# Who issues the stores of the second mixer's projections: SyncE, or ScalarE and GpSimd

## Chip, core and metric

The kernel runs on one core of a Trainium2 chip. The metric is the time of one execution on the device in microseconds (us), and the median over several runs is given. A profile of one execution shows every instruction of five engines: TensorE (PE, its weight loads PEld), VectorE (DVE), ScalarE (ACT), GpSimd (POOL) and SyncE (SP). An instruction that starts a transfer (DMA) stands in the queue of the engine that issues it, in that queue's order; its row carries the engine's name with a q (SPq, ACTq).

## What is computed

Two layers of a streaming encoder run over 1104 tokens: a prompt of 16 + 1024 and a sample of 64. Layer 0 mixes tokens with a gated delta rule, layer 1 with RWKV-7 time mixing; each mixer is followed by a gated feed-forward network. The change lies in layer 1's mixer, whose projections are:

```python
xx = h_prev - h
xr, xw, xk, xv, xa, xg = h[None] + xx[None] * mu[:, None, None, :]
r, k, v = xr @ w_r, xk @ w_k, xv @ w_v
w_log = -softplus(-(w0 + tanh(xw @ w1) @ w2)) - 0.5
a = sigmoid(a0 + (xa @ a1) @ a2)
gate = sigmoid(xg @ g1) @ g2
kk = l2_normalize(heads(k * k_k))
k = k * (1.0 + (a - 1.0) * k_a)
decay = exp(-exp(w_log))
...
S = S * d_t + (S @ -kk_t) * b_t + v_t * k_t      # token by token, in the kernel by chunks of 64
bonus = sum(r * k * r_k, heads) * v
```

All is float32; a product of matrices is made of three passes over a high and a low part of each operand.

## The kernel before

Activations lie with the 1024 channels on 8 tiles f of 128 partitions and tokens along the row, in three groups g of 336, 384 and 384 tokens (`FULL`). The mixer has two halves. `rwkv_a` computes the projections and writes them, one tile of 128 x 384 per (f, g), to scratch tensors in DRAM: R, SW (the sigmoid that gives the decay), A, PQ (running decay), KR (two planes: scaled kk and scaled r), BK (two planes: scaled a*kk and k), V, BV (bonus) and GT (gate). `rwkv_b` reads them back by batches of heads and runs the chunked recurrence.

The stages of `rwkv_a` in order:

- `dense(0)`: receptance, with `store` writing R (L1265). VectorE copies the tile out of PSUM for odd f, ScalarE for even f. Woven into it run the low-rank projections `lora`; their second stage writes SW (L1252) and A (L1265), both made by ScalarE.
- `dense(2)` with `post_k`: per tile it loads A (L1391) and SW (L1401), normalises the key with one more matmul (L1405), scans the decay on VectorE (L1414), makes three exponentials on ScalarE (pe, pi, pq: L1416 to L1418), copies a column block of pq on GpSimd (plb, L1419), and stores PQ (L1421), KR[0] (L1423), BK[0] (L1426) and BK[1] (L1428). The last three are VectorE's products pe, bh, kh. Their tiles have two buffers each.
- `dense(3)` with `post_v`: per tile it loads PQ, BK[1] and R (L1455 to L1457), multiplies on VectorE (rt L1458, kh L1460), sums per head with a matmul (L1462), copies V out of PSUM on ScalarE (L1464), multiplies it (pq, L1466), and stores KR[1] (L1459), V (L1465) and BV (L1467). pq, kh and rt have two buffers each, and so has ev. Woven into it run the first steps of the recurrence's first batch: `grams`, `inverse` (a substitution whose columns VectorE and GpSimd share, L599 and L601; transposes L1602, L1605 after it) and `build` (loads L1553 to L1556).
- `gates`: loads the gate's hidden rows (L1150), four matmuls per tile (L1166), a copy on ScalarE (go, L1168, two buffers), and the store GT (L1169). All but its start runs beside the first batch of `rwkv_b`.

`mix` (L1219 to L1240) makes the shifted input of each projection and splits it into high and low part; GpSimd writes one column (md, L1236) where the sample starts. Weights come by `wunit` (L117), 512 KB each.

In the text of the kernel every one of these loads and stores is issued by `nc.sync`. The order of instructions on each queue is not the program's: a planner orders them by priorities and its own estimate of durations, and adds the semaphores. `weave(*gens)` only interleaves the program order of several generators by given weights.

Of the kernel before, what the change touches and what calls it, by code (L numbers as in the profile page):

```python
# [11 lines left out]
AF = mybir.ActivationFunctionType  # L12
# [40 lines left out]
def tile_trunk(ctx, tc, *aps, stages=("gdn", "ffn0", "rwkv", "ffn1"), dbg=None):  # L53
    nc = tc.nc
# [1088 lines left out]
    def gates(tp, xp, dr):  # L1143
        w2 = ins["rwkv_g2"][0]
        hid = []
        for i in range(3):
            t = tp.tile([P, T], F32R, tag=f"hg{i}", bufs=1, name=uid("hg"))
            for c0, n in FULL:
                x = xp.tile([P, 384], F32, tag="ev", name=uid("hx"))
                nc.sync.dma_start(x[:, :n], dr["HG"][i, :, c0:c0 + n])  # L1150
                nc.scalar.copy(t[:, c0:c0 + n], x[:, :n])
            yield
            hid.append(t)
        raws = [rep2(w2[0:128], 1), rep2(w2[128:160], 4)]
        h, l, h2 = (tp.tile([P, KT, P], F32R, tag=f"g2{i}", bufs=1, name=uid("g2")) for i in range(3))
        split(h.rearrange("p a b -> p (a b)"), l.rearrange("p a b -> p (a b)"), raws[0])
        hf = h2.rearrange("p a b -> p (a b)")
        nc.scalar.copy(hf, raws[1])
        nc.vector.tensor_tensor(hf[64:128], raws[1][64:128], hf[64:128].bitcast(F32), ALU.subtract)
        terms = [(h, hid[0]), (h, hid[1]), (l, hid[0]), (h2, hid[2])]  # L1160
        yield
        for f in range(8):
            for g, (c0, n) in enumerate(LIVE):
                ps = psC()
                for i, (w, x) in enumerate(terms):
                    nc.tensor.matmul(ps[:, :n], w[:, f], x[:, c0:c0 + n], start=i == 0, stop=i == 3)  # L1166
                o = tp.tile([P, 384], F32, tag="go", bufs=2, name=uid("go"))
                nc.scalar.copy(o[:, :n], ps[:, :n])  # L1168
                nc.sync.dma_start(dr["GT"][f, :, (g + 1) * 384 - n:(g + 1) * 384], o[:, :n])  # L1169
                yield  # L1170

    def hand_over(tp, xT, c0, n):
# [23 lines left out]
    def rwkv_a(hnp, col, prm, pc, plb, dr, esb, esx, esg, pend, esP):  # L1196
        C = math.exp(-0.5)
        with ExitStack() as es0, ExitStack() as es:
# [4 lines left out]
            o = pc["rwkv_mu"]  # L1203
            nc.vector.tensor_scalar(omu, prm[:, o:o + 48], -1.0, 1.0, ALU.mult, ALU.add)
            ka1 = rp.tile([P, 8], F32, name="ka1")
            o = pc["rwkv_k_a"]
# [35 lines left out]
            def store(ps, n, g, f, name, func=AF.Copy, bias=0.0):  # L1242
                if name == "SW":
                    i = 2 if g else 1
                    e = (sv1 if g else sv0)[cnt[i] % 2]
                    cnt[i] += 1
                    if g == 0:
                        nc.scalar.activation(e[:, 0, 49:65], ps[:, 0:16], func, bias=bias)
                        nc.scalar.activation(e[:, 1:6, 1:65], ps[:, 16:n].rearrange("p (c t) -> p c t", t=64), func, bias=bias)
                    else:  # L1250
                        nc.scalar.activation(e[:, :, 1:65], ps[:, :n].rearrange("p (c t) -> p c t", t=64), func, bias=bias)
                    nc.sync.dma_start(dr["SW"][f, :, 6 * g:6 * g + 6], e)  # L1252
                else:
                    if g == 0:
                        e = ev0[cnt[0] % 2]
                        cnt[0] += 1
                    else:
                        e = mp.tile([P, 384], F32, tag="ev", name=uid("ev"))
                    if func == AF.Copy and f % 2:
                        nc.vector.tensor_copy(e[:, 384 - n:], ps[:, :n])  # L1260
                    elif func == AF.Copy:
                        nc.scalar.copy(e[:, 384 - n:], ps[:, :n])
                    else:
                        nc.scalar.activation(e[:, 384 - n:], ps[:, :n], func, bias=bias)
                    nc.sync.dma_start(dr[name][f, :, g * 384:(g + 1) * 384], e)  # L1265

            def dense(s, w, post):
                m = [None] * 3
# [128 lines left out]
            def post_k(ps, n, g, f):  # L1397
                o = 384 - n
                A = load("l0", "A", f, g)
                sw = tmp("sw", [P, 390])  # L1400
                nc.sync.dma_start(sw, dr["SW"][f, :, 6 * g:6 * g + 6].rearrange("p a b -> p (a b)"))  # L1401
                sq = tmp("sq")
                nc.scalar.activation(sq[:, :n], ps[:, :n], AF.Square, scale=col("rwkv_k_k", f))
                pn = psC()
                nc.tensor.matmul(pn[:, :n], bd1, sq[:, :n], start=True, stop=True)  # L1405
                nc.scalar.activation(sq[:, :n], pn[:, :n], AF.Ln, bias=eps_t)
                nc.scalar.activation(sq[:, :n], sq[:, :n], AF.Exp, scale=-0.5)
                kk, k2 = (kk0[f % 2], k20[f % 2]) if g == 0 else (tmp("kk"), tmp("k2"))
                nc.vector.scalar_tensor_tensor(kk[:, o:], ps[:, :n], col("rwkv_k_k", f), sq[:, :n], ALU.mult, ALU.mult)
                nc.scalar.activation(k2[:, o:], A[:, o:], AF.Identity, scale=col("rwkv_k_a", f), bias=ka1[:, f:f + 1])  # L1410
                nc.vector.tensor_tensor(k2[:, o:], k2[:, o:], ps[:, :n], ALU.mult)
                nc.vector.tensor_tensor(A, A, kk, ALU.mult)
                l = sw.rearrange("p (c t) -> p c t", t=65)
                nc.vector.tensor_tensor_scan(sw, sm.rearrange("p a b -> p (a b)"), sw, 0.0, ALU.mult, ALU.add)  # L1414
                pe, pi, pq = tmp("pe"), tmp("pi"), tmp("pq")
                nc.scalar.activation(c3(pe), l[:, :, 0:64], AF.Exp, scale=-C)  # L1416
                nc.scalar.activation(c3(pi), l[:, :, 1:65], AF.Exp, scale=C)
                nc.scalar.activation(c3(pq), l[:, :, 1:65], AF.Exp, scale=-C)  # L1418
                nc.gpsimd.tensor_copy(plb[:, f, 6 * g:6 * g + 6], c3(pq)[:, :, 63])  # L1419
                cs = slice(g * 384, (g + 1) * 384)  # L1420
                nc.sync.dma_start(dr["PQ"][f, :, cs], pq)  # L1421
                nc.vector.tensor_tensor(pe, kk, pe, ALU.mult)
                nc.sync.dma_start(dr["KR"][0, f, :, cs], pe)  # L1423
                bh, kh = tmp("bh"), tmp("kh")
                nc.vector.tensor_tensor(bh, A, pi, ALU.mult)
                nc.sync.dma_start(dr["BK"][0, f, :, cs], bh)  # L1426
                nc.vector.tensor_tensor(kh, k2, pi, ALU.mult)
                nc.sync.dma_start(dr["BK"][1, f, :, cs], kh)  # L1428

            for i, (dst, c) in enumerate(((p_shift, SPL), (s_shift, T))):  # L1430
                t8 = tp.tile([P, 8], F32, tag="t8", bufs=1, name=f"t8{i}")
# [13 lines left out]
            with ExitStack() as es, ExitStack() as es1:  # L1445
                set_wp(es, 2, 3)
                mp = pool(es, "rm3", 2)
                mdb[0] = 2
                mp0 = pool(es1, "rm0", 2)

                def post_v(ps, n, g, f):
                    o = 384 - n
                    cs = slice(g * 384, (g + 1) * 384)
                    pq, kh, rt = (mp.tile([P, 384], F32, tag=t, name=uid(t)) for t in ("pq", "kh", "rt"))
                    nc.sync.dma_start(pq, dr["PQ"][f, :, cs])  # L1455
                    nc.sync.dma_start(kh, dr["BK"][1, f, :, cs])
                    nc.sync.dma_start(rt, dr["R"][f, :, cs])  # L1457
                    nc.vector.tensor_tensor(rt, rt, pq, ALU.mult)  # L1458
                    nc.sync.dma_start(dr["KR"][1, f, :, cs], rt)  # L1459
                    nc.vector.scalar_tensor_tensor(kh, rt, col("rwkv_r_k", f), kh, ALU.mult, ALU.mult)  # L1460
                    pn = psC()
                    nc.tensor.matmul(pn[:, :384], bd1, kh, start=True, stop=True)  # L1462
                    e = ev0[f % 2] if g == 0 else mp.tile([P, 384], F32, tag="ev", name=uid("ev"))
                    nc.scalar.copy(e[:, o:], ps[:, :n])  # L1464
                    nc.sync.dma_start(dr["V"][f, :, cs], e)  # L1465
                    nc.vector.tensor_tensor(pq, pn[:, :384], e, ALU.mult)  # L1466
                    nc.sync.dma_start(dr["BV"][f, :, cs], pq)  # L1467

                d = dense(3, ins["rwkv_w_v"][0], post_v)
                for _ in range(4):  # L1470
                    next(d)
                Bx.home(flat(hnp.rearrange("p a b -> p (a b)")))
                weave((8, upto(8, d)), (D1, then(Bx.grams(0), Bx.inverse(0))))
                weave((8, upto(8, d)), (D2, Bx.build(0, 0)))
                es1.close()
                gts = gates(pool(esg, "rg", 2, side="right"), mp, dr)
                weave((4, d), (4, upto(4, gts)))
            return Bx, gts
# [399 lines left out]
    if "gdn" in stages:  # L1878
        dr = {k: dp_.tile([9, P, 8, P], F32, name="d" + k) for k in ("KN", "VB", "KD", "QG", "TT", "QK", "SZ")}
        dr["G"] = dp_.tile([9, 8, P], F32, name="dG")  # L1880
        with ExitStack() as es:
# [4 lines left out]
            with ExitStack() as es2:  # L1886
# [14 lines left out]
                with lnexp_tables():  # L1901
                    load_x(xT, ready)
                    nc.sync.dma_start(dx, xT)
                    for g in range(3):
                        n = FULL[g][1]
# [103 lines left out]
```

## Time and profile before

| | |
|---|---|
| median of 3 runs | 3351.06 us (3349.12 to 3355.72) |
| profiled execution | 3353.38 us, span 3351.6 us |
| granted TensorE clock, mean | 0.974 |
| instructions | 69660 |
| moved by DMA | 452.49 MB, mean 135 GB/s |
| share of the busiest queue (q1) | 445.61 MB |

The span is the time from the first to the last instruction of the profile. The stages that the diff touches lie between about 1598 and 2160 us. Busy time of an engine counts its own instructions, not waits and not the issuing of DMAs. A wait row names the waiting instruction, what ended the wait, the total in us, how many times, and the longest. In a row of one source line, durations are in ns as minimum/median/maximum, then first and last start in us.

### The profile page before, as it was taken

How to read it: one execution, taken by the hardware profiler on the slowest of the kernel's cores; microseconds unless marked ns; L12 is line 12 of the kernel's file. 1: busy time of each engine (PE TensorE's matmuls, PEld its weight loads, DVE VectorE, ACT ScalarE, POOL GpSimd, SP SyncE). 2: the span in 40 equal slices, each digit the busy share in tenths (PEclk: the TensorE clock that was granted, in tenths of full speed). 3: DMA queues.
4: the chain of work that ended last, by engine and by line, in shares of the span. 5: the costliest groups of instructions: out<-in, count | busy, mean ns of one | idle time of the engine just before them, and what ended most of it. 6: DMA issues, size and time to landing. Idle time of an engine off the chain costs nothing. (4 is left out here: it accounts for less than half of the span.)

```text
span 3351.6 us, 69660 instructions
## 1 busy us (share of the span) xinstructions
PE 3177.9 (95%) x27426; PEld 2983.6 (89%) x27426; DVE 2505.8 (75%) x5011; ACT 1561.5 (47%) x3134; POOL 293.1 (9%) x539
## 2 busy tenths in 40 slices
PE   7999999898999999999999888888999999999998
PEld 6888888798999999999998777677778999999998
DVE  6967867467777667766879874889986687877775
ACT  5866766434433333213778733434455443333112
POOL 1000000002200000000001130533300310000000
PEclk9999999999999999999999999989999999999999
DMA  5433332884332225422256876445565333335231
GB/s 167 118 99 101 105 91 71 293 278 138 97 98 82 78 75 169 131 83 88 76 184 194 279 227 211 134 141 164 161 192 170 105 97 97 94 94 175 85 98 61
DMA packets 543912, 452.49 MB, mean 135 GB/s; under 512 B 78377, under 2 KB 494930, under 8 KB 543458
## 3 DMA queue, kind: packets, MB, share of 16 engines
q1 hardware_dynamic: 538682, 445.61, 43.2%
q8 instruction: 216, 3.54, 0.4%
q10 hardware_dynamic: 4904, 2.43, 0.3%
q14 instruction: 110, 0.90, 0.1%
HBM read 306.86 MB, written 141.07 MB: 134 GB/s over the span
## 5 line engine op out<-in xcount | busy, mean ns | idle before, releaser
L311 PE MATMUL psA<-tc,sh 128*128 128x276 f32 (+1 forms) x1712 | 500.2, 292 | 20.4 <-DVE hs L319 9.4
L313 PE MATMUL psA<-tc,sl 128*128 128x276 f32 (+1 forms) x1712 | 499.9, 292 | 4.0 <-DVE sl L110 3.9
L312 PE MATMUL psA<-tc,sh 128*128 128x276 f32 (+1 forms) x1712 | 499.4, 292 | 0.3 <-DVE tc L110 0.2
L407 DVE TENSOR_TENSOR xT<-xT,psA 128x384 f32<-128x384 f32 (+3 forms) x496 | 252.4, 521 | 135.0 <-PE psA L132 133.2
L311 PEld LDWEIGHTS psA<-tc,sh 128*128 128x128 f32 x1712 | 327.0, 191 | 22.6 <-DVE hs L319 10.1
L109 ACT CAST wh<-raw 128x1024 fp32r<-128x1024 f32 x159 | 166.3, 1049 | 357.8 <-PE psA L131 239.9
L313 PEld LDWEIGHTS psA<-tc,sl 128*128 128x128 f32 x1712 | 326.5, 191 | 5.0 <-DVE sl L110 4.7
L312 PEld LDWEIGHTS psA<-tc,sh 128*128 128x128 f32 x1712 | 326.6, 191 | 1.2 <-DVE tc L110 0.9
L131 PE MATMUL psA<-hl,wh 128*128 128x384 f32 (+3 forms) x1024 | 326.4, 319 | 0.0
L130 PE MATMUL psA<-hh,wh 128*128 128x384 f32 (+3 forms) x1024 | 325.7, 320 | 0.0
L132 PE MATMUL psA<-hh,wl 128*128 128x384 f32 (+3 forms) x1024 | 325.3, 318 | 0.0
L130 PE MATMUL psA<-hnh,wh 128*128 128x384 f32 (+1 forms) x768 | 269.9, 351 | 5.4 <-ACT hnh L109 4.1
L131 PE MATMUL psA<-hnl,wh 128*128 128x384 f32 (+1 forms) x768 | 262.3, 341 | 1.7 <-DVE hnl L110 1.7
L132 PE MATMUL psA<-hnh,wl 128*128 128x384 f32 (+1 forms) x768 | 261.0, 340 | 0.0
L110 DVE TENSOR_TENSOR wl<-raw,wh 128x1024 fp32r<-128x1024 f32 x159 | 195.0, 1228 | 66.0 <-ACT wh L109 65.5
L109 ACT CAST sh<-raw 128x512 fp32r<-128x512 f32 x202 | 124.9, 621 | 254.9 <-PE psA L312 235.0
L130 PE MATMUL psA<-mxh,wh 128*128 128x384 f32 (+1 forms) x672 | 225.0, 345 | 10.6 <-ACT mxh L109 5.6
L131 PE MATMUL psA<-mxl,wh 128*128 128x384 f32 (+1 forms) x672 | 229.7, 344 | 1.9 <-DVE mxl L110 1.6
L132 PE MATMUL psA<-mxh,wl 128*128 128x384 f32 (+1 forms) x672 | 226.8, 339 | 0.3 <-DVE wl L110 0.3
L130 PEld LDWEIGHTS psA<-hh,wh 128*128 128x128 f32 x1024 | 192.0, 188 | 0.6 <-ACT hh L109 0.4
L132 PEld LDWEIGHTS psA<-hh,wl 128*128 128x128 f32 x1024 | 192.4, 188 | 0.1
L131 PEld LDWEIGHTS psA<-hl,wh 128*128 128x128 f32 x1024 | 192.2, 188 | 0.3
(490 smaller groups left out, 8204.3 us busy)
## 6 DMA issues: line engine op xcount, KB each, us to landing
raw<-in_ffn_w_gate_dram SPq DMA_DIRECT2D x64, 512.0 KB
raw<-in_ffn_w_up_dram SPq DMA_DIRECT2D x64, 512.0 KB
raw<-in_ffn_w_down_dram SPq DMA_DIRECT2D x44, 512.0 KB
raw<-in_gdn_w_in_dram SPq DMA_DIRECT2D x32, 512.0 KB
raw<-in_gdn_w_out_dram SPq DMA_DIRECT2D x24, 512.0 KB
raw<-in_rwkv_w_o_dram SPq DMA_DIRECT2D x24, 512.0 KB
hr<-dhid SPq DMA_DIRECT2D x44, 276.0 KB
hr<-dhid SPq DMA_DIRECT2D x44, 272.0 KB
```

The costliest lines, as they stand in the source:

```text
L109: nc.scalar.copy(h, src)
L110: (eng or nc.vector).tensor_tensor(l, src, h.bitcast(F32), ALU.subtract)
L130: nc.tensor.matmul(ps, w[0][:, k, :], x[0][:, k, :n], start=a, stop=False)
L131: nc.tensor.matmul(ps, w[0][:, k, :], x[1][:, k, :n], start=False, stop=False)
L132: nc.tensor.matmul(ps, w[1][:, k, :], x[0][:, k, :n], start=False, stop=z)
L311: nc.tensor.matmul(ps, u[0][:, kk], h, start=first and kk == 0, stop=False)
L312: nc.tensor.matmul(ps, u[0][:, kk], l, start=False, stop=False)
L313: nc.tensor.matmul(ps, u[1][:, kk], h, start=False, stop=last and kk == 3)
L407: nc.vector.tensor_tensor(xT[:, m, a:a + n], xT[:, m, a:a + n], pd[:, :n], ALU.add)
```

## The change

Only the engine that issues a store is changed, in `gates`, `store`, `post_k` and `post_v`; no load, tile or computation is. Stores of tiles that ScalarE wrote go to ScalarE's queue: GT, SW, A, R of even f, PQ, V. Stores of VectorE's tiles go to GpSimd's queue: KR[0], BK[0], BK[1], KR[1], BV. R of odd f, which VectorE copies, stays with SyncE.

```diff
@@ gates
-                nc.sync.dma_start(dr["GT"][f, :, (g + 1) * 384 - n:(g + 1) * 384], o[:, :n])
+                nc.scalar.dma_start(dr["GT"][f, :, (g + 1) * 384 - n:(g + 1) * 384], o[:, :n])
@@ store
-                    nc.sync.dma_start(dr["SW"][f, :, 6 * g:6 * g + 6], e)
+                    nc.scalar.dma_start(dr["SW"][f, :, 6 * g:6 * g + 6], e)
...
-                    if func == AF.Copy and f % 2:
+                    q = nc.sync if func == AF.Copy and f % 2 else nc.scalar
+                    if q is nc.sync:
                         nc.vector.tensor_copy(e[:, 384 - n:], ps[:, :n])
...
-                    nc.sync.dma_start(dr[name][f, :, g * 384:(g + 1) * 384], e)
+                    q.dma_start(dr[name][f, :, g * 384:(g + 1) * 384], e)
@@ post_k
-                nc.sync.dma_start(dr["PQ"][f, :, cs], pq)
+                nc.scalar.dma_start(dr["PQ"][f, :, cs], pq)
                 nc.vector.tensor_tensor(pe, kk, pe, ALU.mult)
-                nc.sync.dma_start(dr["KR"][0, f, :, cs], pe)
+                nc.gpsimd.dma_start(dr["KR"][0, f, :, cs], pe)
                 bh, kh = tmp("bh"), tmp("kh")
                 nc.vector.tensor_tensor(bh, A, pi, ALU.mult)
-                nc.sync.dma_start(dr["BK"][0, f, :, cs], bh)
+                nc.gpsimd.dma_start(dr["BK"][0, f, :, cs], bh)
                 nc.vector.tensor_tensor(kh, k2, pi, ALU.mult)
-                nc.sync.dma_start(dr["BK"][1, f, :, cs], kh)
+                nc.gpsimd.dma_start(dr["BK"][1, f, :, cs], kh)
@@ post_v
-                    nc.sync.dma_start(dr["KR"][1, f, :, cs], rt)
+                    nc.gpsimd.dma_start(dr["KR"][1, f, :, cs], rt)
...
-                    nc.sync.dma_start(dr["V"][f, :, cs], e)
+                    nc.scalar.dma_start(dr["V"][f, :, cs], e)
                     nc.vector.tensor_tensor(pq, pn[:, :384], e, ALU.mult)
-                    nc.sync.dma_start(dr["BV"][f, :, cs], pq)
+                    nc.gpsimd.dma_start(dr["BV"][f, :, cs], pq)
```

## The prediction

> **What bounds the kernel now.** I read the page's head, its queue part and its chain first.
>
> ```profile
> span 3351.6 us, 69660 instructions
> q1 hardware_dynamic: 538682, 445.61, 43.2%
> PE 30%; DVE 6%; DMA 1%; issue 1%; ACT 1%; POOL 0%; SPq 0%; DVEq 0%; ACTq 0%; POOLq 0%
> ```
>
> TensorE carries the chain (PE 30%). Nearly all bytes (445.61 MB) go through one queue, q1, which is SyncE's. No row shows a transfer that GpSimd issued. Over the whole span SP's own issuing (SPq) is 0% of the chain, so the stages that the diff touches decide. The view of busy time by windows gives them: length, then busy us (and counts) of PE, PEld, DVE, ACT, POOL, then granted clock, DMA share, GB/s.
>
> ```profile
> 1598.00:1765.00 167.00, 160.55 (x915) 153.80 (x914) 134.50 (x273) 124.61 (x268) 13.58 (x38) 0.99 0.41 131
> 1765.00:1895.00 130.00, 118.54 (x628) 105.75 (x625) 120.16 (x224) 111.33 (x233) 19.11 (x33) 0.99 0.73 236
> 1895.00:2062.00 167.00, 148.01 (x1149) 127.14 (x1150) 112.44 (x223) 65.01 (x128) 33.71 (x70) 0.93 0.79 243
> 2062.00:2160.00 98.00, 84.56 (x1544) 70.03 (x1543) 71.64 (x171) 42.00 (x99) 31.71 (x71) 0.89 0.48 136
> ```
>
> In order: receptance and low-rank stage (PE-bound); key stage (DVE busy 120.16 of 130); value stage (PE idle 19.0); gates with the first batch (PE idle 13.4). All PE idle together is 50.3 us (562 less 511.65), the most that any relief could bring. Next, the waits inside these windows: who waited, for what, total us, times, longest.
>
> ```profile
> PE psC L1462 <- DVE kh L1460: 10.5, 8, 2.3
> PE psA L130 <- ACT wh L109: 4.8, 1, 4.8
> DVE rt L1458 <- DMA pq<-rPQ: 13.8, 7, 5.1
> DVE sw L1414 <- DMA sw<-rSW: 3.5, 4, 1.5
> ```
>
> The first three are of the value stage: PE waits for kh, kh for rt, rt for the load of pq. The last is the key stage's. So a late load costs something in the value stage, little before it.
>
> **The change, part by part.** It takes 252 stores off SP: 132 to ScalarE (GT 24, SW 24, A 24, PQ 24, V 24, R of even f 12) and 120 to GpSimd (KR 48, BK 48, BV 24). R of odd f, 12 stores, stays on SP. Bytes and loads stay. Prices of one issue, from the rows of single lines (min/median/max ns, first and last start) and of the timeline:
>
> ```profile
> L1169 SPq DMA_DIRECT2D rGT<-go x24: 319/537/1442, 2060.9 to 2155.4; - x24
> 581.04 0.51 ACT L225 ACTIVATE sg<-sg 128x384 f32<-128x384 f32 x1
> 581.17 0.37 ACTq L972 DMA_DIRECT2D dTT<-tfp  x1
> 581.58 0.53 ACT L226 ACTIVATE sg<-sg 128x384 f32<-128x384 f32 x1
> ```
>
> *Relief of SP, value stage start.* PE stands 4.8 us at the first weight. SP reached that load only after the wait of a PQ store:
>
> ```profile
> 1887.95 0.42 SPq L1391 DMA_DIRECT2D l<-rA  x1
> 1890.04 0.32 SPq L1421 DMA_DIRECT2D rPQ<-pq  x1
> 1890.41 0.43 SPq L117 DMA_DIRECT2D raw<-in_rwkv_w_v_dram  x1
> ```
>
> From 1888.4 (end of the load) to 1890.4 SP stood or issued that store: 2.0 us. Ends: 0, if the raw tile's memory was not free, and 4.8. I take 2.0, the row's own: **-2.0**.
>
> *Relief, value stage loop.* SP's own waits there:
>
> ```profile
> SPq L1459 <- DVE rt L1458: 13.0, 12, 3.1
> SPq L1465 <- ACT ev L1464: 10.2, 11, 2.2
> SPq L1467 <- DVE pq L1466: 9.1, 10, 3.1
> SPq L1455 <- DMA rBV<-pq: 6.5, 12, 1.1
> ```
>
> SP stands 32.3 us before the three stores, and loads queue behind. But at 12 of the 24 loads of pq SP itself was waiting for the BV store to leave the buffer (two buffers): these cannot come earlier. So half of PE's 10.5 us is out of reach; of the other 5.2 I take half, **-2.6** (ends 0 and -5.2).
>
> *Relief, key stage.* DVE, its bound, waits 3.5 us for sw; a third, **-1.2** (ends 0 and -3.5). In the low-rank stage PE is busy 160.55 of 167, and no load of it stands among the waits above: 0 (at most the 6.4 us of PE's idle time there).
>
> *Relief, gates.* SP issues nearly back to back, GT stores among the loads; the chain of waits runs through it:
>
> ```profile
> 2147.99 1.44 SPq L1169 DMA_DIRECT2D rGT<-go  x1
> ...
> 2060.92 2.90 DMA rGT<-go
> 2078.31 3.25 DMA k<-rKR
> 2149.47 0.57 SPq L1553
> 2150.09 0.61 SPq L1553
> 2150.75 3.47 DMA xT<-rKR
> ```
>
> 24 issues at the median 0.537 give SP 12.9 us back. On the chain stand 10.8 us of transfer and issue (the five rows); a transfer's own time stays, so the gain is what SP was late: the store of 1.44 ahead of 2149.47, and I put as much again for the other two places: **-3.0** (ends 0 and -10.8).
>
> *ScalarE's 132 issues.* Each costs at most 0.37 and a turnaround that I put at 0.1, where nothing else runs, and next to nothing where an instruction runs meanwhile (the issue at 581.17 lies inside L225, which ends at 581.55; the next starts at 581.58). At a mean 0.2, 60 stores (SW, A, R) put 12 us on ACT's 124.6 of 167, and 24 PQ stores 5 us on 111.3 of 130: covered by PE's 160.6 and DVE's 120.2, though tightly. **+2.5** for copies that come a little later on the chain (ends 0, and 132 x 0.47 = 62 on ACT, of which the key stage would pass DVE by 111.3 + 11.3 - 120.2 = 2.4 and the low-rank stage 0). ACT writes these tiles itself, so its stores wait only for ACT; nothing foreign blocks its queue.
>
> *GpSimd's 120 stores.* One such store's price on POOL is shown nowhere. Ends: 0.32 (the shortest of SP's row) and 2.06, POOL's longest row in these stages. The nearest is an instruction of POOL's own over 128 partitions, 1.03, and I take that.
>
> ```profile
> L1419 POOL COPY plb<-pq x24: 193/403/2056, 1768.2 to 1891.3; 128x6 f32<-128x6 f32 x24
> L1419 POOL COPY plb<-pq 128x6 f32<-128x6 f32 x24 | 14.2, 594 | 119.9 <-ACT pq L1418 119.9
> L1236 POOL TENSOR_TENSOR md<-prm 128x1 f32<-128x1 f32 x16 | 7.7, 481 | 39.2 <-DVE mxl L110 39.0
> L1598 POOL MEMSET b32t<- 128x1024 f32 x2 | 2.1, 1026 | 15.8 <-DVE b32tn L1605 13.4 <-DMA rBK<-kh 2.4
> L1427 DVE TENSOR_TENSOR kh<-k,pi x24: 547/551/556, 1784.8 to 1896.7; 128x384 f32<-128x384 f32 x24
> ```
>
> Key stage: a round takes (1896.7 - 1784.8)/23 = 4.87 us. POOL's round becomes 3 x 1.03 + 0.59 (plb) + 0.32 (md, 7.7/24) = 4.0: covered, **0**. POOL becomes the bound from (4.87 - 0.91)/3 = 1.32 us a store; each 0.1 above costs 0.1 x 3 x 23 = 6.9 us. The last round's stores leave about 1.7 us later (3 x (1.03 - 0.45)), and the value stage reuses that memory (POOL's MEMSET L1598 already waits 2.4 us for rBK<-kh): **+1.5** (ends 0 and 3 x 1.6 = 4.8). The md columns of both stages (16) queue behind stores that wait for DVE: **+1.0** (ends 0 and 16 x 1.03).
>
> Value stage: BV and KR[1] sit on rings of two buffers; each of 11.5 turns grows by 1.03 - 0.32 = 0.7. Half of them bind (12 of 24 above): **+4.1** (ends -1, as stores no longer queue on SP, and 11.5 x 1.74 = 20). The Trainium skill, DMA: Bandwidth & Descriptors, Specifications, gives a first byte after about 1 us for a GpSimd store against 0.6 for SyncE's or ScalarE's; by that 0.4 this term would be 2.3, and no run here shows it yet. POOL also does part of the first inverse in this stage:
>
> ```profile
> L599 POOL TENSOR_TENSOR b32w<-b32a,b32t x158: 228/468/767, 1946.4 to 2426.4; 128x27 f32<-128x27 f32 x10, 128x52 f32<-128x52 f32 x10, 128x75 f32<-128x75 f32 x10, 128x96 f32<-128x96 f32 x10
> 1971.77 0.24 POOL L601 TENSOR_TENSOR b32t<-b32t,b32w 128x23 f32<-128x23 f32 x1
> 1981.11 0.17 DVE L601 TENSOR_TENSOR b32t<-b32t,xT 128x8 f32<-128x8 f32 x1
> L1458 DVE TENSOR_TENSOR rt<-rt,pq x24: 544/557/837, 1904.9 to 2052.9; 128x384 f32<-128x384 f32 x24
> ```
>
> POOL starts it at 1946.4 and ends 9.3 us before DVE's part. Rounds of (2052.9 - 1904.9)/23 = 6.4 us put 4 rounds, 8 stores, 8.2 us, into it: just covered. **+1.0** for stores that hold POOL while DVE makes rt and pq (ends 0 and 8 x 2.06 - 9.3 = 7.2); when late, DVE's transpose L1602 and PE behind it stand.
>
> *Sum.* -2.0 - 2.6 - 1.2 - 3.0 = -8.8; +2.5 + 1.5 + 1.0 + 4.1 + 1.0 = +10.1; together +1.3. The profiled execution took 3353.4 (span 3351.6 and 1.8 around it): 3354.7. It lies 2.3 above the median of 3351.1, so the forecast for the median is **3352.4: no measurable change**. A difference under 0.2%, 6.7 us, cannot be told from none here.
>
> **Rivals.** *Faster: the stores were what made the loads late.* If GpSimd's stores leave as soon as SP's did and ACT hides its own, the costs vanish and the relief doubles: half of PE's 15.3 us in the value stage (7.7), all 3.5 of the key stage, half the 10.8 of the gates: -16.6, 3334. SP's waits of 32.3 us speak for it; the 12 loads that wait for a landing speak against. Chance 0.26.
>
> *Slower: the ring of two buffers in the value stage.* A BV store that lands later makes the load of pq, rt, kh and PE's L1462 later at every turn. With all turns bound and 1.5 us a store: 11.5 x 1.18 = 13.6 instead of 4.1, and the loop's relief of 2.6 gone: +13.4, 3364.5. It decides (past +6.7) from 0.92 us if every turn binds. For it: PE's 10.5 us wait is this very chain; against: half the turns have slack. Chance 0.18.
>
> *Slower: POOL becomes the key stage's bound.* At 1.6 us a store, 2.8 x 6.9 = +19.3: 3372. POOL's plb copies, 193 ns at best and 594 on average beside a DVE that is 92% busy, show that POOL is held up there. Chance 0.18. The Trainium skill, SBUF — State Buffer, SBUF: two separate sides, says that a GpSimd store's descriptors cannot be written while VectorE holds the shared port, and a later section there has 620 ns alone and about 3100 beside a tensor_copy; at 3.1 us this rival would be +123. The same page, Who interferes with whom, exempts tensor_tensor, which is most of what DVE runs here, so I give the long price little weight.
>
> *The change moves more than it says.* Queues are not filled in program order: R's stores, the first stage's, still run 20 us after the key stage's first loads.
>
> ```profile
> L1265 SPq DMA_DIRECT2D rR<-ev x24: 319/320/1073, 1598.5 to 1766.9; - x24
> L1401 SPq DMA_DIRECT2D sw<-rSW x24: 320/442/1205, 1746.6 to 1886.0; - x24
> ```
>
> So the planner may place other work anew; I count that both ways inside the range, and as no case of its own.
>
> **Chances.** The forecast keeps 0.38, and is the "same" case; faster 0.26; slower 0.18 + 0.18 = 0.36. The range goes down to 3336, nearly the faster rival, and up to 3376, past both slower ones; the forecast's own range is 3344.4 to 3357.8.
>
> **What would show it.** SP's waits at L1459, L1465 and L1467 gone, PE's first weight of the value stage earlier by about 2 us, SP less dense after 2062. POOL rows of DMA issue with a duration: under 1.32 us the key stage keeps 130 us, above it grows. PE's wait for kh in the value stage: under 10.5 us the ring did not bind, above 15 it did. POOL's last L601 of the first inverse before DVE's. I am wrong if a POOL store takes 1.5 us or more, or if ACT's issues make PE wait in the first stage.

## The result: 1.3% slower

The changed kernel took 3391.27 us (median; 3387.0 to 3395.3) against 3350.09 for the kernel before on the same chip: ratio 1.013, 95% interval 1.0114 to 1.0146. The prediction, 3352.4 with a range up to 3376, was wrong, and both of its slower rivals were too small.

From here on, lines after L1259 carry a number one higher in the changed kernel: its L1266 is L1265 before, its L1468 is L1467. The head of its page, queues and chain:

```profile
span 3393.2 us, 69701 instructions
q1 hardware_dynamic: 502394, 396.24, 38.5%
q10 hardware_dynamic: 23912, 28.21, 2.4%
q0 software_dynamic: 7680, 23.60, 1.8%
PE 28%; DVE 8%; issue 4%; DMA 3%; POOL 2%; ACT 1%; SPq 0%; DVEq 0%; ACTq 0%; POOLq 0%
```

The change did what it says: q1 lost 49.4 MB (445.61 before), and ScalarE's q10 and GpSimd's q0 carry it. In the chain POOL went from 0% to 2%, DMA from 1% to 3%, issue from 1% to 4%.

Where the time went is seen best in a table by stage. I cut both spans at the same events: ScalarE's first copy of R, the first key matmul (L1405), the first value matmul (L1462), the first gate matmul (L1166), the last one, the end. The view by windows, before and then after (columns as in the prediction):

```profile
1597.20:1780.30 183.10, 173.35 (x984) 165.40 (x983) 148.29 (x301) 139.38 (x300) 13.97 (x39) 0.98 0.42 132
1780.30:1909.10 128.80, 116.64 (x603) 103.83 (x602) 118.66 (x217) 105.56 (x218) 22.12 (x39) 0.96 0.78 253
1909.10:2056.00 146.90, 134.09 (x1100) 115.51 (x1098) 98.25 (x196) 53.44 (x107) 28.52 (x58) 0.97 0.77 236
2056.00:2152.20 96.20, 81.50 (x1433) 66.73 (x1434) 67.35 (x161) 41.99 (x97) 27.82 (x62) 0.89 0.50 145
2152.20:3351.60 1199.40, 1135.92 (x11492) 1069.65 (x11492) 934.29 (x1859) 463.97 (x894) 144.51 (x258) 0.97 0.41 124
```

```profile
1600.50:1805.30 204.80, 182.11 (x985) 172.60 (x984) 148.26 (x300) 143.81 (x298) 13.79 (x39) 0.93 0.37 118
1805.30:1946.30 141.00, 118.72 (x581) 104.12 (x580) 115.89 (x212) 102.45 (x212) 59.01 (x112) 0.91 0.69 226
1946.30:2117.00 170.70, 144.29 (x1120) 124.02 (x1118) 99.53 (x202) 57.85 (x115) 53.25 (x104) 0.92 0.70 217
2117.00:2208.70 91.70, 77.13 (x1434) 63.77 (x1430) 67.87 (x162) 42.31 (x97) 29.20 (x63) 0.93 0.58 169
2208.70:3393.00 1184.30, 1121.95 (x11493) 1058.11 (x11492) 931.38 (x1858) 462.59 (x893) 148.07 (x258) 0.98 0.40 123
```

Receptance stage +21.7, key stage +12.2, value stage +23.8, gates -4.5, all behind them -15.1; the part ahead of the first cut, where nothing differs, +3.3. Together 41.4 of the spans' 41.6.

Read the first row of each block. Three engines are less busy per microsecond after, and no engine is the bound: 182.11 of 204.80 on PE, 148 on DVE, 144 on ACT. Time that no engine uses is waiting, so the next view is PE's waits for `mxh` from 1590 to 1790 us, before and after (the stage after runs on to 1805, and has 15.8 us in all):

```profile
PE psA L130 <- ACT mxh L109: 2.9, 3, 1.5
```

```profile
PE psA L130 <- ACT mxh L109: 15.0, 8, 4.1
```

The matmuls stand before `mxh`, ScalarE's cast of the mixed input. Why it is late is in ScalarE's timeline just ahead of the worst wait (PE stands 4.1 us up to 1685.1):

```profile
1682.10 0.58 ACT L1251 ACTIVATE sv<-psA,prm 128x384 f32<-128x384 f32 x1 [0.17 <-DMA rSW<-sv]
1683.55 0.58 ACT L1251 ACTIVATE sv<-psA,prm 128x384 f32<-128x384 f32 x1 [0.87 <-DMA rSW<-sv]
1683.61 0.88 ACTq L1252 DMA_DIRECT2D rSW<-sv  x2
1684.53 0.51 ACT L109 CAST mxh<-md 128x384 fp32r<-128x384 f32 x1 [0.40 <-ACT sv L1251]
```

The cast that PE needs stands behind a run of `sv` sigmoids. The two shown wait until the store of an earlier one has left its buffer (0.17 and 0.87 us), and the cast then waits 0.40 us while ScalarE issues a store. That is 1.4 of the 4.1 us; in the rest ScalarE works through other instructions that stand ahead of the cast. Nor did the waits for those buffers grow: they are 1.5 us in the stage, before and after. Two causes are mixed here: the order in which the instructions stand, and the issues. The program asks for the same instructions in both; the planner placed 385 of TensorE's 22198, 310 of VectorE's 5011 and 230 of ScalarE's 3131 elsewhere (the fewest moves that turn one order into the other).

A hole here can cost more than its own length. PE's idle time in the stage grew from 9.75 us (183.10 less 173.35) to 22.69, by 12.9; the other 8.8 us is the same matmuls taking longer, 182.11 against 173.35, at a granted clock of 0.93 instead of 0.98. By windows of 5 us around two holes (PE idle 4.14 us up to 1685.1 and 3.50 up to 1703.1):

```profile
1680.00:1685.00 5.00, 0.83 (x3) 0.31 (x3) 1.24 (x3) 3.06 (x8) 0.00 (x0) 0.95 0.74 242
1685.00:1690.00 5.00, 4.91 (x15) 4.51 (x16) 4.93 (x11) 3.40 (x8) 0.00 (x0) 0.50 0.11 42
1690.00:1695.00 5.00, 5.00 (x29) 5.00 (x29) 3.73 (x9) 2.58 (x6) 0.81 (x2) 0.87 0.00 0
...
1700.00:1705.00 5.00, 1.88 (x5) 1.58 (x6) 2.35 (x6) 4.21 (x12) 0.26 (x1) 0.66 0.46 169
1705.00:1710.00 5.00, 5.00 (x22) 4.84 (x21) 5.00 (x13) 3.46 (x8) 1.54 (x4) 0.66 0.00 2
```

After the first hole the clock is 0.50, and 15 matmuls start in a window where the next one has 29 at 0.87. The Trainium skill, TensorE: Matmul & The Clock Gate, Part 1: The HAM clock gate, says that the clock falls to half after an idle window of about 3.4 us and comes back after as long a busy one; this trace agrees, with 0.50 behind that hole of 4.14 us.

In the key stage PE waits for `sq`, ScalarE's square of the key, before and after:

```profile
PE psC L1405 <- ACT sq L1403: 4.7, 5, 1.6
```

```profile
PE psC L1406 <- ACT sq L1404: 14.7, 12, 4.1
```

That is 10.0 of the stage's 12.2 us.

The value stage has its own mechanism. Rows of VectorE, GpSimd, SyncE and TensorE around its longest hole:

```profile
1992.44 0.55 DVE L1467 TENSOR_TENSOR pq<-psC,ev 128x384 f32<-128x384 f32 x1
...
2001.10 0.44 POOL L599 TENSOR_TENSOR b32w<-b32a,b32t 128x143 f32<-128x143 f32 x1
2001.57 0.58 POOL L1468 DMA_DIRECT2D rBV<-pq  x1
2002.17 0.47 POOL L601 TENSOR_TENSOR b32t<-b32t,b32w 128x143 f32<-128x143 f32 x1
...
2003.77 0.32 SPq L1456 DMA_DIRECT2D pq<-rPQ  x1
...
2006.18 0.56 DVE L1459 TENSOR_TENSOR rt<-rt,pq 128x384 f32<-128x384 f32 x1 [6.01 <-DMA pq<-rPQ]
2007.15 0.81 DVE L1461 SCALAR_TENSOR_TENSOR kh<-rt,prm,kh 128x384 f32<-128x384 f32 x1
2008.02 1.65 PE L1463 MATMUL psC<-kh,bd 128*128 128x384 f32 x2 [7.52 <-DVE kh L1461]
```

`pq` was ready at 1992.99. Its store left GpSimd at 2001.57, 8.6 us later, between two column steps of the inverse; GpSimd works through its queue in order and had a row of them ahead. SyncE could load the next `pq` into that buffer only at 2003.77, so rt, kh and TensorE followed, with a hole of 7.5 us. Over the stage SyncE's wait for BV to land, 6.5 us before (the prediction's row of L1455), became:

```profile
SPq L1456 <- DMA rBV<-pq: 36.0, 15, 7.5
```

Pairing the 24 products with the 24 stores in order of time, three BV stores left 8.6, 11.4 and 6.2 us after their data and the others within 2.3; of KR[1] three left 8.8, 8.4 and 3.7 us after, the others within 2.9. Before, the longest such delay was 0.8 for BV and 3.2 for KR[1].

### The profile page after: what moved, and what is told of

The parts are those of the page before. It is cut to its first block, busy times and chain, and to the rows that moved or that the text cites. A ratio compares the mean times of both kernels' runs of the same rounds, so it can differ in the third digit from the quotient of the medians.

```text
span 3393.2 us, 69701 instructions
## 1 busy us (share of the span) xinstructions
PE 3184.3 (94%) x27426; PEld 2988.4 (88%) x27426; DVE 2501.7 (74%) x5011; ACT 1564.9 (46%) x3134; POOL 359.4 (11%) x659
## 5 line engine op out<-in xcount | busy, mean ns | idle before, releaser
L109 ACT CAST sh<-raw 128x512 fp32r<-128x512 f32 x202 | 124.6, 619 | 254.8 <-PE psA L312 233.8
L132 PEld LDWEIGHTS psA<-hh,wl 128*128 128x128 f32 x1024 | 192.5, 188 | 0.1
```

The costliest lines, as they stand in the source:

```text
L109: nc.scalar.copy(h, src)
L132: nc.tensor.matmul(ps, w[1][:, k, :], x[0][:, k, :n], start=False, stop=z)
```

## Experiments

Two theories: **P**, the planner's new order of the compute instructions takes the time; **H**, the stores cost it on their new queues. To separate them I hold the order. The planner takes edges that fix the order of issue and add no wait, so the instructions of TensorE, VectorE, ScalarE and GpSimd can be made to stand as in another kernel:

```python
# names: the compute instructions of one engine, in the other kernel's order
for ins, prev in zip(names[1:], names):
    tc.add_manual_dep(here[ins], prev, NoSync)      # issue order only
```

DMAs are not held, and so SyncE's own order still changes: in `p_after_queues` 264 of its DMAs stand elsewhere than before (counted as above). No run holds a kernel to its own order, so what holding itself does is not measured. The table gives the median, the ratio to the kernel before with its interval, and the lengths of the stages in the one profile of each kernel.

| kernel | us | ratio (95%) | receptance | key | value | gates | rest |
|---|---|---|---|---|---|---|---|
| before | 3349 to 3352 | 1 | 183.1 | 128.8 | 146.9 | 96.2 | 1199.4 |
| changed | 3391.3 | 1.013 (1.0114-1.0146) | 204.8 | 141.0 | 170.7 | 91.7 | 1184.5 |
| p_after_queues | 3368.9 | 1.0062 (1.0044-1.0079) | 192.2 | 127.7 | 161.4 | 92.0 | 1198.6 |
| p_before_queues | 3402.2 | 1.0175 (1.0152-1.0198) | 200.9 | 155.9 | 159.5 | 102.6 | 1187.0 |
| e_act | 3360.5 | 1.0041 (1.0024-1.0058) | 203.0 | 133.1 | 152.4 | 91.1 | 1190.4 |
| e_pool | 3365.4 | 1.0050 (1.0031-1.0069) | 185.2 | 132.8 | 179.7 | 90.8 | 1191.3 |
| p_kr1bv_sp | 3355.1 | 1.0010 (0.9999-1.0020) | 193.0 | 128.3 | 152.9 | 90.6 | 1191.0 |
| p_first_sp | 3359.2 | 1.0031 (1.0020-1.0043) | 183.1 | 128.7 | 160.9 | 91.6 | 1198.1 |
| p_kr1bv_act | 3359.7 | 1.0033 (1.0020-1.0046) | 192.5 | 128.8 | 156.6 | 91.1 | 1193.0 |
| e_gt | 3336.0 | 0.9950 (0.9936-0.9964) | 182.9 | 128.2 | 152.2 | 94.8 | 1186.9 |
| p_gt | 3343.2 | 0.9988 (0.9975-1.0001) | 181.8 | 128.8 | 148.6 | 94.5 | 1190.7 |
| b_gtorder | 3364.6 | 1.0052 (1.0033-1.0070) | 183.8 | 128.4 | 149.3 | 123.4 | 1193.5 |
| g_pqv | 3343.2 | 0.9986 (0.9974-0.9999) | 181.4 | 130.3 | 155.0 | 91.1 | 1189.1 |
| g_key | 3340.5 | 0.9975 (0.9961-0.9988) | 182.2 | 129.2 | 154.3 | 90.7 | 1189.8 |
| a_hold1 | 3387.8 | 1.0106 (1.0088-1.0125) | 192.5 | 146.0 | 172.7 | 90.4 | 1187.9 |
| e_ra | 3357.4 | 1.0025 (1.0012-1.0037) | 186.6 | 130.3 | 149.2 | 94.5 | 1197.4 |
| e_sw | 3368.6 | 1.0061 (1.0041-1.0081) | 201.5 | 129.0 | 144.3 | 96.3 | 1195.7 |

How far to trust one stage: in the kernels with no edit in it, receptance lies between 181.4 and 185.2, value (no store of the key or value stage moved, and their order as before) between 144.3 and 152.2, and the rest between 1184 and 1199. The part ahead of the stages, where no store was moved, ends between 1590.8 and 1601.1. And a profile shows one execution, which need not be a middling one: `e_pool`'s took 3379.2 us against a median of 3365.4, `b_gtorder`'s 3373.1 against 3364.6, `e_gt`'s 3343.2 against 3336.0, `e_sw`'s 3359.3 against 3368.6.

**Order against queues.** `p_after_queues`: the full change, compute held to the order before.

> The changed kernel with its stores on ScalarE's and GpSimd's queues, but the order of all compute instructions on TensorE, VectorE, ScalarE and GpSimd held to that of the kernel before (ordering edges only). SyncE's loads and the places of the stores stay the planner's. Theory P (the planner put the compute instructions in another order, and that order costs the 41 us): 3345 to 3362 us, and the receptance stage is back within 5 us of before's. Theory H (the stores cost what they cost on their new queues: issue time, waits in front of them, later landings): 3380 to 3395, with the receptance stage still some 20 us longer and the value stage some 20 us longer. In between: both, in the measure of where it lies.

`p_before_queues`: no store moved, compute held to the order of the full change.

> The mirror image: all stores stay with SyncE as in the kernel before, but the compute instructions of the four engines are held to the order that the planner made for the changed kernel. Theory P: 3380 to 3400 us, with the receptance stage some 20 us longer than before's. Theory H: 3345 to 3358, no measurable change.

Neither end was hit by the first: 3368.9 lies between, so both causes are there. The second gave 3402.2 with every store still on SyncE: the order alone is enough for a loss of this size (SyncE's order goes with it: 332 of its 1744 DMAs stand elsewhere than before). PE's waits for `mxh` in the receptance stage, of `p_before_queues` and then `p_after_queues`:

```profile
PE psA L130 <- ACT mxh L109: 13.8, 6, 4.1
```

```profile
PE psA L130 <- ACT mxh L109: 6.4, 9, 3.2
```

With the new order and no store on ScalarE it is 13.8 us; with the old order and the stores there 6.4; before 2.9. ScalarE's timeline in `p_before_queues`, and then at the same place in the kernel before:

```profile
1685.94 0.58 ACT L1251 ACTIVATE sv<-psA,prm 128x384 f32<-128x384 f32 x1 [1.21 <-DMA rSW<-sv]
1687.27 0.58 ACT L1251 ACTIVATE sv<-psA,prm 128x384 f32<-128x384 f32 x1 [0.74 <-DMA rSW<-sv]
...
1690.03 0.58 ACT L1251 ACTIVATE sv<-psA,prm 128x384 f32<-128x384 f32 x1 [0.33 <-DMA rSW<-sv]
1690.51 0.50 ACT L109 CAST mxh<-md 128x384 fp32r<-128x384 f32 x1
```

```profile
1689.17 1.06 ACT L1251 ACTIVATE sv<-psA,prm 128x384 f32<-128x384 f32 x2
...
1691.09 0.94 ACT L109 CAST mxh<-md 128x384 fp32r<-128x384 f32 x2
1692.28 1.13 ACT L1251 ACTIVATE sv<-psA,prm 128x384 f32<-128x384 f32 x2
...
1693.75 0.50 ACT L109 CAST mxh<-md 128x384 fp32r<-128x384 f32 x1
```

In the new order the cast that PE wants stands behind a run of sigmoids and other work and comes at 1690.51, where a hole of 3.8 us ends (1691.06). Waiting for the `sv` buffers is the smaller part of it: of the three waits shown only the last, 0.33 us, falls into the hole. In the old order the casts stand between pairs of sigmoids.

The key stage's whole loss goes with the order (127.7 held, 141.0 not; PE's wait for `sq` is 4.2 us held), the value stage's only in part (161.4). A held order has a price of its own, though: it was made for other queues. The last hole of `p_before_queues`, 14.3 us in the gates, is in neither kernel, so its total is no measure of the order to the microsecond.

**Half the change each.** `e_act`: ScalarE's 132 stores. `e_pool`: GpSimd's 120. The planner is free in both.

> Only ScalarE's 132 stores moved (GT, SW, A, R of even f, PQ, V); the 120 of VectorE's tiles stay with SyncE. The planner orders freely. Theory H with ScalarE's issues as the cost in the receptance stage and GpSimd's stores as the cost in the key and value stages: receptance stage +20, key and value stage within 5 of before's, gates some 5 shorter: 3360 to 3368. Theory P: 356 of TensorE's 22198 instructions stand elsewhere than before, nearly as many as in the full change (385), so also the key and value stages are longer: 3370 to 3390.

> Only GpSimd's 120 stores moved (KR, BK, BV); the 132 of ScalarE's tiles stay with SyncE. The planner orders freely. Theory H: receptance stage as before, key stage +12 and value stage +24 as in the full change: 3380 to 3390. Theory P: 220 of TensorE's instructions stand elsewhere; the time is set by where, and lies below that of the full change: 3350 to 3375.

Receptance +20 with ScalarE's stores alone and +2 with GpSimd's, value stage +5.5 and +32.8 (of these +5.5 is hardly outside the spread, and +32.8 is from an execution 14 us over its median). The receptance loss comes with ScalarE's stores and most of the value loss with GpSimd's, as H had it by stage, though with a free planner this does not part issues from order; of the totals `e_act`'s is in H's range, `e_pool`'s in P's. The key stage lost only 4 us in each, 12 in both together.

**Which stores, at a fixed order.** `p_after_queues` with KR[1] and BV on SyncE (`p_kr1bv_sp`), with the receptance stage's stores on SyncE (`p_first_sp`), or with KR[1] and BV on ScalarE (`p_kr1bv_act`):

> The changed kernel with compute held to the order before, as in p_after_queues (3368.9 us, value stage 161.4 us against 146.9 before), but KR[1] and BV, the two stores of the value stage, back on SyncE. Theory Q (on GpSimd these two stand behind the column steps of the inverse, leave late, and the loads into the same two-buffer tiles wait for their landing: SyncE waited 33.5 us for BV and 28.2 for KR there, against 6.5 and 3.1 before): value stage back within 4 us of 146.9, SyncE's two waits under 12 us, total 3352 to 3360. Rival (it is the planner's new order of SyncE's loads, or the key stage's late stores): value stage stays over 155, total 3363 to 3372.

> The changed kernel with compute held to the order before, but the 60 stores of the receptance stage (SW, A, R of even f) back on SyncE. Receptance stage: 192.2 us in p_after_queues, 183.1 before. Theory A (ScalarE's issues and the wait of its sv for the SW landing delay the mxh casts): back to 182 to 186, TensorE's wait for mxh from 6.4 back to 2.9 us, total 3358 to 3364. Rival (order of SyncE's loads): stays near 192, total 3365 to 3372.

> As p_kr1bv_sp, but KR[1] and BV on ScalarE's queue instead of SyncE's, so still off SyncE and not behind GpSimd's inverse. Theory Q: value stage 140 to 150 us, total 3350 to 3360. Rival (any store that leaves SyncE lets the loads and stores of one ring lose their order, whichever engine takes it): value stage over 155, total 3363 to 3372.

The clearest result is `p_first_sp`: 183.1 us, exactly before's stage, and the wait for `mxh` at 2.6. So at the old order ScalarE's 60 stores cost 9 us. The order of SyncE's loads, the rival, is out: apart from the 60 stores, one DMA of SyncE stands elsewhere than in `p_after_queues`. `p_kr1bv_sp` brought 3355.1, no longer told from before, with the value stage at 152.9 (2 us over what was expected, and 0.7 over the spread of the kernels without an edit there); 32 of SyncE's other DMAs stand elsewhere than in `p_after_queues`. On ScalarE the two stores give the total that theory Q asked, 3359.7, but the stage of its rival, 156.6. No KR[1] or BV store stood over 3 us behind its data in it. What remains there I cannot assign.

One expectation was badly made. SyncE's two waits for a landing were to fall under 12 us in `p_kr1bv_sp`; the one for BV stayed at 14.7, the one for KR fell to 6.7. With the two stores on ScalarE they are longer still. `p_kr1bv_act` in the value stage:

```profile
SPq L1456 <- DMA rBV<-pq: 27.0, 12, 5.2
SPq L1457 <- PE psC L1463: 18.4, 12, 3.7
SPq L1458 <- DMA rKR<-rt: 17.2, 13, 3.4
```

Before, SyncE stood before its stores (32.3 us in the prediction's three rows) and then 9.6 before the loads (6.5 for BV, 3.1 for KR). Freed of the stores it stands before the loads instead, for the same buffers: the relief did not shorten its waiting.

**The gates alone.** `e_gt` moves only the 24 GT stores:

```python
-                nc.sync.dma_start(dr["GT"][f, ...], o[:, :n])
+                nc.scalar.dma_start(dr["GT"][f, ...], o[:, :n])
```

> Only the 24 GT stores moved to ScalarE, nothing else; the planner orders freely, and compute then stands elsewhere only from the gates on (126 of TensorE's 22198 instructions), in the batches in the same new order as in the full change. Receptance, key and value stage as before. Theory P (the order decides): gates 4 to 6 us shorter and the batches behind them 8 to 15 us shorter, as in the four kernels in which the planner was free: 3330 to 3341. Rival (the shorter batches came from the stores of the earlier stages, or are noise between executions): 3343 to 3351.

3336.0 us, 0.5% faster than before: it beats both kernels. Theory P has the total; of its stages the gates missed (-1.4 for 4 to 6), and the batches gave 12.5. Where SyncE stood in the gates before, and what issuing the store costs ScalarE in `e_gt`:

```profile
SPq L1169 <- ACT go L1168: 12.0, 7, 4.2
```

```profile
L1169 ACTq DMA_DIRECT2D rGT<-go x24: 326/330/367, 2062.1 to 2155.1; - x24
```

SyncE stood 12.0 us for ScalarE's copies, with the batch's loads behind; that wait is gone. Is it the order or the queue that gains? `p_gt` holds the order before under it, `b_gtorder` puts its order under the queues before:

> Only the 24 GT stores on ScalarE, but all compute held to the order before. e_gt, the same stores with the planner free, took 3336.0 us against 3351.6, most of it in the batches behind the gates (about 10 us) where no store is moved. Theory P (the order makes the gain): 3345 to 3353. Rival (SyncE's loads leave sooner without the GT stores, and that makes the gain): 3333 to 3341.

> The mirror image: every store on SyncE as before, compute held to the order that the planner made for e_gt. Theory P: 3333 to 3343. Rival: 3347 to 3356.

Neither theory. `p_gt` at 3343.2 is between the two forecasts and, by its interval, just not told from before. `b_gtorder` lost 15 us, outside both, with one long wait of PE in the gates:

```profile
PE psB L1562 <- ACT at L1534: 18.6, 1, 18.6
```

SyncE stood 21.7 us before the GT stores there, against 12.0 before. Behind the gates a new order is the shorter one on either queue: 1184.5 to 1193.5 us in the nine profiles that have it, 1190.7 to 1199.4 in the eight that do not. So the whole gain was measured only with queue and order together: with every store on SyncE the gates lose more (27.2 us) than the batches gain. `g_pqv` and `g_key` add PQ and V, then also KR[0] and BK, at `e_gt`'s order:

> GT, PQ and V (72 stores) on ScalarE, compute held to e_gt's order. The relief of SyncE by itself, without a new order: the prediction gave it 2.0 us at the first weight of the value stage and 2.6 in its loop. If that relief is real: 3330 to 3334. If it is hidden: 3334 to 3339. If ScalarE's stores delay V's copies: over 3340.

> As g_pqv, with the key stage's KR[0] and BK (72 stores) on GpSimd as well. With compute held to the order before, the full change left the key stage at 127.7 us against 128.8, so GpSimd's issues of 0.54 us should be covered here too: within 3 us of g_pqv, 3330 to 3340. If GpSimd's later stores make the value stage's first loads wait: 3342 or more.

3343.2 (the range of the third case) and 3340.5 (half a microsecond out of its range): no better than `e_gt`. The relief of SyncE that the prediction counted at the value stage brings nothing that can be measured, and 72 more stores on GpSimd cost nothing in the key stage (129.2). That V's copies were delayed, as the over-3340 case said, is not shown.

**One stage held.** `a_hold1` is the full change with the order held in the receptance stage alone; `e_ra` and `e_sw` move only that stage's A and even R, or only SW.

> The full change, with the order of compute held to that before in the receptance stage alone; from the key stage on the planner's own new order stands. Theory P: the receptance stage goes from 204.8 to about 192 us (its value with all order held; ScalarE's issues keep the rest over 183.1), key and value stage stay as in the full change (141.0 and 170.7): total 3391 less 13, 3373 to 3383. Rival (the stages are not independent, a gain in one is lost in the next): over 3386.

> Only the 36 stores A and R of even f on ScalarE, planner free. 173 of TensorE's instructions stand elsewhere. If these stores turn the receptance stage's order: stage 195 to 205 us against 183.1. If not: 183 to 188.

> Only the 24 SW stores on ScalarE, planner free. 98 of TensorE's instructions stand elsewhere. If the SW stores turn the order (the sv instructions ahead of the mxh casts): stage 193 to 203 us. If not: 183 to 188.

The stage went to 192.5, as told, but the total only to 3387.8, which is the rival's: key stage +5.0, value stage +2.0 and the rest +3.4 took most of it back. The stages are not independent, and my account of 41 us by stage is a description of one trace, not a sum of separate prices. SW's 24 stores turn the receptance stage's order (201.5, against 186.6 for A and R): in `e_sw` PE waits for `mxh`

```profile
PE psA L130 <- ACT mxh L109: 17.0, 7, 7.1
```

as much as in the full change. The number of moved instructions does not decide: in that stage A and R move 81 of TensorE's, SW 98. Why the planner's estimate puts the sigmoids ahead of the casts once ScalarE stores them, no run shows.

## Why the prediction was wrong

- **The planner's order as no case of its own.** This step failed first. I wrote that the planner may place other work anew, both ways inside the range. It did, in every kernel in which it was free. Holding compute to the order before took 22 of the 41 us back (3391.3 to 3368.9), and at that order the key stage had no loss at all. The 19 us that stay come with the stores of the next two steps: put back on SyncE, those of the receptance stage took about 10 us off (3359.2), KR[1] and BV about 14 (3355.1). Whether these two add up, no run shows.
- **ScalarE's issues, +2.5.** Mis-sized: 9 us in the receptance stage alone (192.2 against 183.1). I covered ACT's 124.6 + 12 by PE's 160.6, busy time by busy time. What ScalarE pays was less than the 12 us that I put: of the 20.3 us of the 60 issues in `p_after_queues` 13.8 lie under other ScalarE instructions, and 6.5 do not. But some of those stand right ahead of a cast, which then starts 0.40 us later, and PE waits for the casts. Of the 9 us PE's idle time is 5.0, and 4.1 is matmuls that take longer (177.48 against 173.35). A cover by totals says nothing about the one instruction that is next. The sign that I named, ACT's issues making PE wait in the first stage, came true.
- **GpSimd in the value stage, +4.1 and +1.0.** The direction was wrong. I asked how far the stores hold up GpSimd's part of the inverse. Hardly: it took 27.7 us against 25.4 before, and its last L601 started at 2016.5, VectorE's at 2037.7. The cost ran the other way, stores waiting up to 11.4 us behind the inverse. VectorE's part then took 48.7 us against 34.4, as VectorE waits for the late `pq` between its columns (6.01 us in the rows above). The ring that I named then did bind, past my 15 us of PE's wait:

```profile
PE psC L1463 <- DVE kh L1461: 20.3, 8, 7.5
```

  At the old order the stage is 14.5 us longer than before, and 8.5 of that go when the two stores go back to SyncE. The first slower rival had the place; that its size (13.4) is near is luck, for it took the price of one issue on every turn for a delay of 6 to 11 us on a few.
- **GpSimd's price, 1.03 us.** Too high, and its rival in the key stage false:

```profile
L1424 POOL DMA_DIRECT2D rKR<-pe x24: 539/539/752, 1810.0 to 1940.0; - x24
L1468 POOL DMA_DIRECT2D rBV<-pq x24: 539/539/582, 1955.7 to 2121.7; - x24
```

  0.54 us, under my 1.32; key stage 127.7 at the old order. My sign alone would have misled: with the free planner the stage grew to 141.0 at this price. The Trainium skill, SBUF — State Buffer, A bandwidth-pool intuition that's wrong (but worth ruling out), tells of about 3100 ns beside a VectorE copy; no row here is over 752, but VectorE runs no copy in the key stage, so the stage does not test it.
- **Relief.** Not shown. At the first weight of the value stage PE's wait of 4.8 is now 3.2, the longest of two (window of the key stage after):

```profile
PE psA L130 <- ACT wh L109: 5.0, 2, 3.2
```

  But in `e_gt`, where SyncE still issues the PQ store that I blamed, it is 3.3. Gates: -4.5 with the full change, -1.4 with GT alone, -3.0 forecast; `e_pool`, which leaves GT on SyncE, has -5.4, so the gain there does not need GT's move. Loop of the value stage: nothing to see of its 2.6. The time after the gates, -15 in the full change and -12.5 in `e_gt`, I did not count at all; part of it is spread between executions.
- **Holes.** Not in the sum: a wait of PE of 3.5 to 4.1 us lowered the clock behind it to 0.50 to 0.66 (means of 5 us), which no term held.

## What to carry over

Before moving a DMA to another engine, look at what stands ahead of it in that engine's queue at that moment, not at the engine's busy share: a queue that is 30% busy can be solid for 10 us (GpSimd in the value stage: 53 of 171 us, and 11.6 of the 13.2 from 1988.8 to 2002.0). In a kernel that a planner orders, an edit of a queue can be an edit of the order of everything; hold the order to tell the two apart, and count holes in TensorE one by one, as the holes here cost 1.2 (key stage), 1.7 (receptance) and 1.8 times (value) their length. Move the stores that hold up other work (24 here, 0.5% faster), not all of a kind (252, 1.3% slower).

## What the hardware showed

Issuing a store of 128 x 384 float32 took GpSimd 0.54 us (539 to 752 ns over 120) and ScalarE's queue 0.33 (326 to 425 ns in the receptance stage), GpSimd's beside a VectorE that was busy for 116 of the key stage's 141 us. Most of ScalarE's issues lay under its other instructions; a GpSimd store stood in line with the rest. The granted clock fell to 0.50 behind a TensorE hole of 4.1 us, and 40% of the receptance stage's loss (8.8 of 21.7 us) came this way.
